# Weights for TensorE kept 128 bytes further into their buffers, and no 512 wide products

## The chip, the core and the metric

The kernel runs on one core of a Trainium2 chip. The metric is the device time of one execution in microseconds, the median over the runs shown. A core has TensorE (matrix products; PE in the profile, its weight loads PEld), VectorE (DVE), ScalarE (ACT), GpSimd (POOL) and SyncE (SP, which issues the DMAs here). Each works through its own queue in order and waits for the others by semaphores.

## The reference

A decoder trunk of two layers over 256 positions of width 2048, in float32. Layer 0 is a recurrent block (RG-LRU), layer 1 sliding-window attention with 32 query heads over 4 shared K/V heads; each is followed by a SwiGLU FFN of inner width 5632.

```python
def swiglu_ffn(x, g, w_in, w_out):
    h = rms_norm(x, g)
    gate, up = jnp.split(h @ w_in, 2, axis=-1)
    return x + (jax.nn.silu(gate) * up) @ w_out
...
    y_branch, x_branch = jnp.split(h @ w_in, 2, axis=-1)
    xb = causal_depthwise_conv(x_branch, conv_w, conv_b)
    hs = rg_lru(xb, w_rg, b_rg, w_ig, b_ig, lam)
    return x + (hs * jax.nn.gelu(y_branch)) @ w_out
...
    for layer in range(DEPTH):
        if layer < N_REC:
            x = recurrent_block(...)
        else:
            if layer == N_REC:
                k_band, v_band = shared_kv(x, kv_norm_g, w_kv, k_norm_g)
            x = attn_block(x, ..., k_band, v_band)
        x = swiglu_ffn(x, norm2_g[layer], ffn_w_in[layer], ffn_w_out[layer])
```

## The kernel before

Activations lie transposed: 128 features on the partitions, 256 positions along the free axis. A float32 number is used as a high part, rounded for TensorE's float32r format, and a low part, the rest. A product of weights W and activations X is then three products: high W with high X ("a" in the code), high W with low X ("b"), low W with high X ("l").

Weights come as tiles of 128x1024 (256 inputs by 512 outputs, 4096 bytes a partition), one DMA each on SyncE's queue into one of four raw buffers. `split` makes hi (ScalarE, line 363) and lo (VectorE, line 364) of it in one of four pairs of buffers; this runs three tiles ahead of TensorE. A job is one such tile: `stream` issues its load, the split of a later tile, then its products, and then as much background work (norms, gates, attention) as fits a budget of VectorE and ScalarE time. The order of all instructions is so fixed when the program is built.

Kinds of jobs:

- A plain group (`group`, products at line 411) has the 128x128 blocks of hi and lo as the stationary weights and the activations as the moving operand, 256 columns wide. A group is four banks (four blocks of 128 outputs) over all inputs; one weight tile gives 24 products, a group over 2048 inputs 192. The LRU's input projections, its output projection, FFN groups 0 to 3 and every second one from 5 on, and the FFN's output projection are such groups. Line 944 (the LRU's gates), line 578 (the attention's output projection in two of its groups, by turns with the heads) and line 1139 (K) use hi and lo as weights in the same way.
- A fast group (`fast_group`, line 606; FFN groups 4, 6, ... 20) saves products by Strassen-like sums (`mix`, lines 374 to 380). There hi and lo, and mixtures of them in slots, move, and the activations in slots are the stationary weights.
- In Q (line 1333) and V (lines 1148 to 1150) hi and lo move too, and the activations are the weights.

Runs of wide products: in the jobs that `sync` names (`SYNC`, mostly the first three of a group), three of the 16 pairs "a" and "b" are issued as one product "h" of 512 columns, high and low X side by side, one behind another. Its second half goes to columns 256 to 511 of the bank. So the first two banks of such a group hold two halves, and whoever reads them adds the halves: a copy by ScalarE into a tile t, an add by VectorE (`pull`, `residual`). 26 groups have such runs, 9 wide products each, and the first group has two more.

Where things lie in a partition matters to the change. SBUF tiles are laid out in the order in which `__init__` makes them. From hi0 to the last slot every tile's size is a multiple of 1024 bytes, but for a tile "step" of 64 bytes between slots 6 and 7. With r for the remainder of hi0's address by 512, all of hi and lo and the near slots (0 to 6) begin at r, the far slots (7 to 36) at r + 64. A 128x128 block of weights is 512 bytes, a 256 wide operand 1024 bytes, so every block and every half of a slot keeps its tile's remainder. Activations are taken from far slots; `mix` takes near slots for its results where job entry 2 is 1, and far slots where it is 2 (tiles 0 and 4 of a group). While a product runs, the weights of the next are loaded. "Spacing" below is the remainder by 512 of the address of those next weights less that of the running product's moving operand: -64 in the plain groups, +64 or (with a mixture in a far slot) 0 in the fast ones.

```python
self.jobs.append((src(c), mm, False))     # a job: source, products, 1 or 2 if mixed
...
run = [(0, 0), (1, 0), (0, 1)] if c in sync else []
todo = [(k, f, p) for k, f in both if (k, f) not in run for p in "ab"]
...
if i == self.NEAR:
    const.tile([P, 16], F32, name="step")
```

Of the kernel before, what the change touches and what calls it, by code (L numbers as in the profile page):

```python
# [49 lines left out]
class Trunk:  # L50
# [12 lines left out]
    SYNC = (0, 1, 2)  # L63
# [13 lines left out]
    def __init__(self, ctx, tc, dram):  # L77
# [276 lines left out]

    def split(self, i):
        raw, hi, lo = self.raw[i % 4], self.hi[i % 4], self.lo[i % 4]
# [28 lines left out]
    def stream(self):  # L385
        n = len(self.jobs)
        for i in range(-self.LD, n):
# [13 lines left out]
    PARTS = {"h": (1, 0, 2 * T), "a": (1, 0, T), "b": (1, T, 2 * T), "l": (0, 0, T)}  # L401

    def products(self, todo, ps, hi, lo, x2, begun, last):


        for n, (k, f, p) in enumerate(todo):
# [4 lines left out]
            self.nc.tensor.matmul(ps[f][:, 0:c1 - c0], w, x2[k][:, c0:c1], start=f not in begun,  # L411
# [3 lines left out]
    def group(self, src, nk, xs, done, last=False, sync=(), four=False, pre=None):  # L415
# [4 lines left out]
        for c in range(nk // 2):  # L420
            def mm(hi, lo, c=c):
# [23 lines left out]
                if c == nk // 2 - 1:  # L445
                    done([(p, bool(sync) and f < 2) for f, p in enumerate(st["ps"])])
            self.jobs.append((src(c), mm, False))

    def pull(self, bank, o=None, r=None):

        ps, two = bank
        o = self.half() if o is None else o
        if two:
            t = self.t()
            self.a(t, ps[:, T:2 * T])
            self.tt(o, ps[:, 0:T], t, ALU.add)
            if r is not None:
                self.tt(o, o, r, ALU.mult)
        elif r is not None:
# [74 lines left out]
    def residual(self, g, ps, gains, r, out=None, part=None):  # L534
        for f in range(4):
            xt = self.x[g][:, f, :]
            p, two = ps[f]
# [907 lines left out]
```

## Time and profile before

| what | value |
|---|---|
| median of 3 runs | 1959.46 us (1959.16 to 1964.55) |
| span of the profiled execution, first to last instruction | 1958.5 us |
| what lies around the span, against the median | 1.0 us |
| TensorE busy | 1953.4 us (100%) |
| VectorE, ScalarE busy | 1538.3 us (79%), 1142.0 us (58%) |
| read from HBM | 376.06 MB, 195 GB/s over the span |
| granted TensorE clock | 1.000 |

A row of a group reads: line, engine, operation, out<-in by the program's names, shape, xcount | busy us, mean ns of one | idle us before. For TensorE the first input named is the moving operand and the second the weights; "128*128" is the array, "128x256" the moving operand. A row of the timeline reads: start us, length us from the first start to the last end, engine, line, operation, names, shape of the first, xcount, and in brackets idle time before it. A row of the windows reads: stretch, its length, then busy us and in brackets the number of instructions that run in it for TensorE, its weight loads, VectorE, ScalarE and GpSimd, then granted clock, DMA share and GB/s.

### The profile page before, as it was taken

How to read it: one execution, taken by the hardware profiler on the slowest of the kernel's cores; microseconds unless marked ns; L12 is line 12 of the kernel's file. 1: busy time of each engine (PE TensorE's matmuls, PEld its weight loads, DVE VectorE, ACT ScalarE, POOL GpSimd, SP SyncE). 2: the span in 40 equal slices, each digit the busy share in tenths (PEclk: the TensorE clock that was granted, in tenths of full speed). 3: DMA queues.
4: the chain of work that ended last, by engine and by line, in shares of the span. 5: the costliest groups of instructions: out<-in, count | busy, mean ns of one | idle time of the engine just before them, and what ended most of it. 6: DMA issues, size and time to landing. Idle time of an engine off the chain costs nothing.

```text
span 1958.5 us, 40255 instructions
## 1 busy us (share of the span) xinstructions
PE 1953.4 (100%) x16516; PEld 1916.5 (98%) x16516; DVE 1538.3 (79%) x2477; ACT 1142.0 (58%) x1670; POOL 0.2 (0%) x4
## 2 busy tenths in 40 slices
PE   9999999999999999999999999999999999999999
PEld 9999999999999999999998899999999999999999
DVE  7989868989899998545667776798899988954443
ACT  7799756555555566444556775565555655744442
POOL 0000000000000000000000000000000000000000
DMA  7555665556666557555554335656566566666663
GB/s 283 188 184 197 212 218 186 188 200 208 205 203 204 204 196 247 194 194 194 194 185 149 130 119 185 208 188 205 194 205 205 202 208 204 230 205 204 205 205 127
DMA packets 107321, 384.97 MB, mean 197 GB/s; under 512 B 11904, under 2 KB 14080, under 8 KB 107136
## 3 DMA queue, kind: packets, MB, share of 16 engines
q1 hardware_dynamic: 106848, 381.99, 58.0%
q8 instruction: 129, 2.11, 0.4%
q14 instruction: 56, 0.46, 0.1%
q10 hardware_dynamic: 288, 0.40, 0.1%
HBM read 376.06 MB, written 6.29 MB: 195 GB/s over the span
## 4 chain that ended last, share of the span: by engine, by line
PE 95%; DVE 2%; DMA 1%; issue 1%; ACT 0%; DVEq 0%; ACTq 0%
PE b L411 67%; PE b L606 16%; PE b L1333 5%; PE b L578 2%; PE b L944 1%; DMA raw<-in_ffn_in 1%; PE b L1184 1%; DVE lo L364 1%; PE b L1248 1%; PE b L1229 1%; PE b L1139 1%; DVE s L144 0%; DVE lo L379 0%; PE b L802 0%; PE b L1307 0%
## 5 line engine op out<-in xcount | busy, mean ns | idle before, releaser
L411 PE MATMUL b<-s,hi 128*128 128x256 f32 (+1 forms) x7700 | 1021.5, 280 | 0.2
L411 PEld LDWEIGHTS b<-s,hi 128*128 128x128 f32 x7700 | 954.0, 188 | 10.9 <-DVE s L144 0.5
L364 DVE TENSOR_TENSOR lo<-raw,hi 128x1024 fp32r<-128x1024 f32 (+1 forms) x579 | 701.9, 1219 | 310.2 <-ACT hi L363 305.1
L363 ACT ACTIVATE hi<-raw 128x1024 fp32r<-128x1024 f32 (+1 forms) x579 | 607.5, 1055 | 457.9 <-PE b L411 396.5
L411 PE MATMUL b<-s,lo 128*128 128x256 f32 x3968 | 586.3, 276 | 0.0
L411 PEld LDWEIGHTS b<-s,lo 128*128 128x128 f32 x3968 | 512.4, 188 | 0.0
L378 ACT ACTIVATE s<-s 128x1024 fp32r<-128x1024 f32 x126 | 131.9, 1058 | 194.1 <-DVE s L377 194.0
L606 PE MATMUL b<-s,s 128*128 128x256 f32 x1512 | 196.2, 279 | 0.4 <-DVE s L380 0.4
L606 PEld LDWEIGHTS b<-s,s 128*128 128x128 f32 x1512 | 183.1, 189 | 0.6 <-DVE s L380 0.6
L606 PE MATMUL b<-hi,s 128*128 128x256 f32 x1044 | 178.0, 277 | 0.0
L380 DVE TENSOR_TENSOR s<-s,s 128x1024 fp32r<-128x1024 f32 x126 | 153.7, 1220 | 5.9 <-ACT s L378 5.9
L606 PEld LDWEIGHTS b<-hi,s 128*128 128x128 f32 x1044 | 152.4, 188 | 0.0
L606 PE MATMUL b<-lo,s 128*128 128x256 f32 x522 | 132.7, 277 | 0.2 <-DVE lo L364 0.2
L375 DVE TENSOR_TENSOR s<-raw 128x512 f32<-128x512 f32 x126 | 86.5, 686 | 47.0 <-DMA raw<-in_ffn_in 46.8
L135 ACT ACTIVATE s<-s 128x512 fp32r<-128x512 f32 (+3 forms) x177 | 87.4, 522 | 55.8 <-DVE s L144 40.3
L379 DVE TENSOR_TENSOR lo<-raw,hi 128x768 fp32r<-128x768 f32 x126 | 118.5, 951 | 0.0
L374 ACT ACTIVATE hi<-raw 128x768 fp32r<-128x768 f32 x126 | 102.4, 833 | 7.4 <-ACT s L378 3.6
L606 PEld LDWEIGHTS b<-lo,s 128*128 128x128 f32 x522 | 92.7, 188 | 0.4 <-DVE lo L364 0.4
L1333 PE MATMUL b<-hi,s 128*128 128x512 f32 x256 | 84.0, 408 | 0.0
L144 DVE TENSOR_TENSOR s<-s,s 128x512 fp32r<-128x512 f32 (+2 forms) x143 | 75.1, 551 | 1.7 <-ACT s L135 1.7
L135 ACT ACTIVATE s<-b 128x256 fp32r<-128x256 f32 (+4 forms) x132 | 57.5, 468 | 24.7 <-PE b L1248 7.2
L144 DVE TENSOR_TENSOR s<-b,s 128x512 f32<-128x512 f32 (+3 forms) x126 | 63.7, 531 | 4.2 <-ACT s L135 3.0
(117 smaller groups left out, 1208.1 us busy)
## 6 DMA issues: line engine op xcount, KB each, us to landing
raw<-in_ffn_in SPq DMA_DIRECT2D x352, 512.0 KB, 3.4
raw<-in_ffn_out SPq DMA_DIRECT2D x176, 512.0 KB, 4.2
raw<-in_lru_in SPq DMA_DIRECT2D x63, 512.0 KB, 3.6
raw<-in_lru_out SPq DMA_DIRECT2D x32, 512.0 KB, 4.1
raw<-in_w_q SPq DMA_DIRECT2D x32, 512.0 KB, 3.2
raw<-in_w_o SPq DMA_DIRECT2D x32, 512.0 KB, 3.3
raw<-in_gate SPq DMA_DIRECT2D x8, 512.0 KB, 4.2
away<-s SPq DMA_DIRECT2D x8, 512.0 KB, 3.4
```

What stands on the lines that cost most here:

```text
L135: self.nc.scalar.activation(out, in_, func, **kw)
L144: self.nc.vector.tensor_tensor(out, a, b, op)
L363: self.nc.scalar.activation(hi[:, q], raw[:, q], AF.Copy)
L364: self.nc.vector.tensor_tensor(lo[:, q], raw[:, q], hi[:, q].bitcast(F32), ALU.subtract)
L374: act(hi[:, q], raw[:, q], AF.Copy)
L375: tt(two(d[:, 0:2 * T]), two(raw[:, T:3 * T]), raw[:, 0:T].unsqueeze(1).to_broadcast([P, 2, T]), ALU.subtract)
L378: act(mh[:, :], d[:, :], AF.Copy)
L379: tt(lo[:, q], raw[:, q], hi[:, q].bitcast(F32), ALU.subtract)
L380: self.mark = tt(ml[:, :], d[:, :], mh[:, :].bitcast(F32), ALU.subtract)
L411: self.nc.tensor.matmul(ps[f][:, 0:c1 - c0], w, x2[k][:, c0:c1], start=f not in begun, stop=last and all(q[1] != f for q in todo[n + 1:]))
L606: nc.tensor.matmul(st["ps"][b][:, h % 2 * T:(h % 2 + n) * T], x, w, start=b not in st["begun"], stop=True, skip_group_check=True)
L1333: nc.tensor.matmul(st[g][b][:, :], x, q, start=c + kt == 0 and x is xh and q is wh, stop=c == 7 and kt == 1 and q is wl)
```

## The change

- hi and lo become 512 bytes longer (a partition holds 1024 + 128 numbers). `parts` gives the 1024 numbers to use: from number 32 on, 128 bytes in, where the job's third entry is None (hi and lo are stationary weights, and V, which shares its job with K), from 0 where it is a number (fast groups 0, 1 or 2; Q now 0). All hi and lo buffers keep one remainder, 4608 being 9 times 512. The plain groups, lines 578, 944 and 1139 so have the spacing +64, V has -64, fast groups and Q keep theirs. Behind a fast group's last product the next plain weights have the spacing 128, once.
- `SYNC`, `sync`, part "h" and the banks' second halves are gone: 236 products of 512 columns become 472 of 256, and 52 copies on ScalarE and 52 adds on VectorE leave.
- The zero tile of the warm-up products is hi[3]. The tiles in front of hi move by a little.

```diff
+    STEP = 32
-        self.zero = const.tile([P, P + T], F32R, name="zero")
-        self.hi = [const.tile([P, 1024], F32R, name=f"hi{i}") for i in range(4)]
-        self.lo = [const.tile([P, 1024], F32R, name=f"lo{i}") for i in range(4)]
+        self.hi = [const.tile([P, 1024 + P], F32R, name=f"hi{i}") for i in range(4)]
+        self.lo = [const.tile([P, 1024 + P], F32R, name=f"lo{i}") for i in range(4)]
...
+    def parts(self, i):
+        o = 0 if self.jobs[i][2] is not None else self.STEP
+        return (q[i % 4][:, o:o + 1024] for q in (self.hi, self.lo))
...
-                self.jobs[i][1](self.hi[i % 4], self.lo[i % 4])
+                self.jobs[i][1](*self.parts(i))
...
-                    todo[0:4] = [(0, f, "h") for f in range(2)]
...
-                    run = [(0, 0), (1, 0), (0, 1)] if c in sync else []
-                    todo = [(k, f, p) for k, f in both if (k, f) not in run for p in "ab"]
-                    at = sync.index(c) if run else 0
-                    todo[at:at] = [(k, f, "h") for k, f in run]
-                    todo += [(k, f, "l") for k, f in both]
+                    todo = [(k, f, p) for k, f in both for p in "ab"] + [(k, f, "l") for k, f in both]
...
-        if two:
-            t = self.t()
-            self.a(t, ps[:, T:2 * T])
-            self.tt(o, ps[:, 0:T], t, ALU.add)
...
-            if two:
-                t = self.t()
-                self.a(t, p[:, T:2 * T])
-                self.tt(xt, xt, t, ALU.add)
...
-            self.jobs.append((w[g, c], mm, False))       # of queries
+            self.jobs.append((w[g, c], mm, 0))
```

On TensorE, the first tile of layer 0's FFN stood so before (b is a bank, s the activations, hi_77 the weights, numbers are buffers):

```order
L411 MATMUL b_141<-s_2965,hi_77 128x512
L411 MATMUL b_142<-s_2965,hi_77 128x256 x2
L411 MATMUL b_143<-s_2965,hi_77 128x256 x2
L411 MATMUL b_141<-s_2965,hi_77 128x256 x2
L411 MATMUL b_140<-s_2965,hi_77 128x512 x2
L411 MATMUL b_142<-s_2965,hi_77 128x256 x2
L411 MATMUL b_143<-s_2965,hi_77 128x256 x2
L411 MATMUL b_140<-s_2965,lo_81 128x256
```

The bank that comes free last is b_140, and the products into the three others stand ahead of it. In the changed kernel the same place on TensorE (the last bank is b_139, the buffer hi_76):

```order
L416 MATMUL b_140<-s_3002,hi_76 128x256 x2
L416 MATMUL b_141<-s_3002,hi_76 128x256 x2
L416 MATMUL b_142<-s_3002,hi_76 128x256 x2
L416 MATMUL b_139<-s_3002,hi_76 128x256 x4
L416 MATMUL b_140<-s_3002,hi_76 128x256 x2
L416 MATMUL b_141<-s_3002,hi_76 128x256 x2
L416 MATMUL b_142<-s_3002,hi_76 128x256 x2
L416 MATMUL b_139<-s_3002,lo_80 128x256
```

Each 512 wide product has become two of 256 columns; six products go ahead of the last bank where the old order had one wide and six narrow ones.

On VectorE, just ahead of that tile, before: the residual adds of the LRU's last output group (s_137 is a quarter of the residual stream, b the banks, t the copied second halves) and the first activation made of it:

```order
L144 TENSOR_TENSOR s_137<-s_137,b_145 128x256
L144 TENSOR_TENSOR s_137<-s_137,b_146 128x256
L144 TENSOR_TENSOR s_137<-s_137,t_86 128x256
L144 TENSOR_TENSOR s_137<-s_137,b_147 128x256
L144 TENSOR_TENSOR s_137<-s_137,t_87 128x256
L144 TENSOR_TENSOR s_137<-s_137,b_140 128x256
L148 SCALAR_TENSOR_TENSOR s_3639<-s_137,par,s_3639 128x256
```

And in the changed kernel:

```order
L143 TENSOR_TENSOR s_136<-s_136,b_144 128x256
L143 TENSOR_TENSOR s_136<-s_136,b_145 128x256
L143 TENSOR_TENSOR s_136<-s_136,b_146 128x256
L147 SCALAR_TENSOR_TENSOR s_3673<-s_136,par,s_3673 128x256
L143 TENSOR_TENSOR s_136<-s_136,b_139 128x256
```

The two adds of second halves are gone, and the activation stands ahead of the last bank's add.

More of the change, by code (lines that the diff above doesn't have):

```diff
@@ L410, in products, with group @@
             w = (hi if high else lo)[:, k * 512 + f * P:k * 512 + f * P + P]
-            self.nc.tensor.matmul(ps[f][:, 0:c1 - c0], w, x2[k][:, c0:c1], start=f not in begun,
+            self.nc.tensor.matmul(ps[f][:, 0:T], w, x2[k][:, c0:c1], start=f not in begun,
                                   stop=last and all(q[1] != f for q in todo[n + 1:]))
             begun.add(f)
-    def group(self, src, nk, xs, done, last=False, sync=(), four=False, pre=None):
+    def group(self, src, nk, xs, done, last=False, four=False, pre=None):
         st = {}
@@ L445, in mm, with pull @@
                 if c == nk // 2 - 1:
[L446 to L451, printed above, removed]
+                    done(st["ps"])
+            self.jobs.append((src(c), mm, None))
+    def pull(self, ps, o=None, r=None):
         o = self.half() if o is None else o
-        if two:
-            t = self.t()
-            self.a(t, ps[:, T:2 * T])
-            self.tt(o, ps[:, 0:T], t, ALU.add)
-            if r is not None:
-                self.tt(o, o, r, ALU.mult)
-        elif r is not None:
+        if r is not None:
             self.tt(o, ps[:, 0:T], r, ALU.mult)
@@ L536, in residual @@
             xt = self.x[g][:, f, :]
-            p, two = ps[f]
+            p = ps[f]
             h = part or 0
             self.tt(xt, xt, p[:, h * T:h * T + T], ALU.add)
-            if two:
-                t = self.t()
-                self.a(t, p[:, T:2 * T])
-                self.tt(xt, xt, t, ALU.add)
             if part != 0:
@@ L581, in mm @@
                 if c == last:
-                    self.residual(g, [(p, False) for p in ps], gains, r, part=g)
-            self.jobs.append((w[g, c], mm, False))
+                    self.residual(g, ps, gains, r, part=g)
+            self.jobs.append((w[g, c], mm, None))
         for q in (range(last - 1), range(last - 1, last + 1)):
@@ L595, in done @@
                 self.residual(g, ps, gains, r, out)
-            self.group(lambda c, g=g: w[g, c], nk, xs, done, g == 3, () if out is not None and g == 3 else self.SYNC)
+            self.group(lambda c, g=g: w[g, c], nk, xs, done, g == 3)
     def fast_group(self, src, xn, mx, g, done, final):
@@ L813, in ffn @@
             if g < self.PLAIN:
-                self.group(src, ND, xs, start, g == self.PLAIN - 1, self.SYNC, four=True)
+                self.group(src, ND, xs, start, g == self.PLAIN - 1, True)
             elif g in self.FAST:
@@ L818, in ffn @@
                 end = g == self.FAST[-1] + 1
-                self.group(src, ND, xn, direct, g == NH // 2 - 1, (), True, 6 if end else None)
+                self.group(src, ND, xn, direct, g == NH // 2 - 1, True, 6 if end else None)
             if g == 0:
@@ L930, in done @@
                 self.spawn(task())
-            self.group(lambda c: w[4 + g, c], ND, xs, done, sync=self.SYNC if g == 2 else (3, 4, 5) if g == 0 else ())
+            self.group(lambda c: w[4 + g, c], ND, xs, done)
         def gates(n):
@@ L1034, in done @@
                 self.spawn(task())
-            self.group(lambda c: w[g, c], ND, xs, done, g == 3, self.SYNC if g else ())
+            self.group(lambda c: w[g, c], ND, xs, done, g == 3)
         for step in self.ORDER.split():
@@ L1052, in done @@
         def done(ps):
-            k0 = [self.pull((p, False)) for p in ps[:2]]
+            k0 = [self.pull(p) for p in ps[:2]]
             for b in range(2):
@@ L1368, in run @@
         self.spawn(first())
-        nc.vector.memset(self.zero[:, :].bitcast(F32), 0.0)
+        zero = self.hi[3]
+        nc.vector.memset(zero[:, 0:P + T].bitcast(F32), 0.0)
         p = self.bank()
         for _ in range(self.WARM):
-            nc.tensor.matmul(p[:, 0:T], self.zero[:, 0:P], self.zero[:, P:P + T], start=True, stop=True)
+            nc.tensor.matmul(p[:, 0:T], zero[:, 0:P], zero[:, P:P + T], start=True, stop=True)
         self.free_bank(p)
```

25 lines of the change are left out of this document (9 added, 16 removed).

## The prediction

> **What bounds the kernel now.** I read the page's head first, then the groups by form, then stretches of the timeline for the pace of TensorE.
>
> ```profile
> span 1958.5 us, 40255 instructions
> PE 1953.4 (100%) x16516; PEld 1916.5 (98%) x16516; DVE 1538.3 (79%) x2477; ACT 1142.0 (58%) x1670; POOL 0.2 (0%) x4
> PE 95%; DVE 2%; DMA 1%; issue 1%; ACT 0%; DVEq 0%; ACTq 0%
> L411 PE MATMUL b<-s,hi 128*128 128x256 f32 x7464 | 976.5, 276 | 0.1
> L411 PE MATMUL b<-s,lo 128*128 128x256 f32 x3968 | 586.3, 276 | 0.0
> L411 PE MATMUL b<-s,hi 128*128 128x512 f32 x236 | 67.4, 393 | 0.1
> ```
>
> TensorE runs without a break and is 95% of the chain that ended last, so the time is the sum of the distances from one product's start to the next. The 276 ns is one product's passage; products overlap, and what costs is the distance. It is read from stretches in which nothing but 256 wide products runs: width of the window over weight loads started in it.
>
> ```profile
> 7.75:24.01 16.26, 16.26 (x140) 16.25 (x138) 15.76 (x34) 14.61 (x30) 0.00 (x0) 1.00 0.95 380
> 307.64:316.01 8.37, 8.37 (x73) 8.37 (x72) 6.62 (x11) 3.97 (x6) 0.00 (x0) 1.00 0.46 157
> 753.19:758.73 5.54, 5.54 (x50) 5.54 (x48) 5.42 (x10) 3.56 (x6) 0.00 (x0) 1.00 0.57 195
> 1264.70:1274.47 9.77, 9.77 (x84) 9.77 (x84) 7.92 (x12) 5.66 (x8) 0.00 (x0) 1.00 0.50 164
> 765.29:818.78 53.49, 53.49 (x473) 53.49 (x472) 26.03 (x25) 20.89 (x21) 0.00 (x0) 1.00 0.61 198
> ```
>
> The second pair of figures is TensorE's products, the third its weight loads. The last row has 472 products in 53.49 us, 113.3 ns each; the first 138 in 16.26 us, 117.8 ns each. The same instruction with the same shapes has two paces, 4.45 ns apart, at the same granted clock (1.00 in all rows). Where the slow one begins and ends is read here:
>
> ```profile
> 305.74 1.07 PE L411 MATMUL b<-s,lo 128*128 128x256 f32 x8
> 307.08 0.50 PE L523 MATMUL b<-con,sq 128*128 128x1 f32 x4
> 309.41 1.10 PE L411 MATMUL b<-s,lo 128*128 128x256 f32 x8
> 316.01 2.04 PE L411 MATMUL b<-s,hi 128*128 128x512 f32 x13
> 317.89 1.10 PE L411 MATMUL b<-s,lo 128*128 128x256 f32 x8
> 320.66 1.07 PE L411 MATMUL b<-s,lo 128*128 128x256 f32 x8
> 752.63 0.60 PE L802 MATMUL b<-con,s 128*128 128x128 f32 x4
> ```
>
> Eight products take 1.07 us before the norm's small products at 307 us, (1.07 - 0.28) / 7 = 113 ns, and 1.10 us after them, 117 ns. The slow pace outlasts the group and the first run of 512 wide products (three of the 13 at 316 us) and is gone behind the second. The window at 753 us begins behind the transposes at 752.63 us in the same way. So a disturbance starts it and, in the lines that keep the weights in hi and lo, only the wide runs or a fast group end it.
>
> By the layout in the code, the product's moving tile and the weights loaded beside it stand -64 bytes apart (modulo 512; next weights minus moving tile) in all of these lines. Two other spacings occur. In fast groups hi and lo move and slots are the weights: +64, and 0 where the second mixture lies in a far slot.
>
> ```profile
> 381.46 1.60 PE L606 MATMUL b<-s,s 128*128 128x256 f32 x12
> L606 PE MATMUL b<-hi,s 128*128 128x256 f32 x1044 | 178.0, 277 | 0.0
> 389.15 0.39 PE L606 MATMUL b<-lo,s 128*128 128x256 f32 x2
> 391.19 0.39 PE L606 MATMUL b<-lo,s 128*128 128x256 f32 x2
> 430.84 0.50 PE L606 MATMUL b<-lo,s 128*128 128x256 f32 x2 [0.21 <-DVE lo L364]
> 431.18 0.62 PE L606 MATMUL b<-hi,s 128*128 128x256 f32 x4
> 431.86 0.62 PE L606 MATMUL b<-hi,s 128*128 128x256 f32 x4
> ```
>
> At 0 it is (1.60 - 0.28) / 11 = 120 ns. At +64, 18 products lie between 389.15 and 391.19 us: 113.3 ns, although 120 ns went before. After the stall at 430.84 us, six products take 431.86 - 431.18 = 0.68 us: 113 ns at once. So at +64 the fast pace comes back by itself where at -64 the slow one stays. The shared K/V stage has both in turn: its K products at -64, its V products at +64.
>
> ```profile
> 1001.50 0.40 PE L1139 MATMUL b<-s,hi 128*128 128x256 f32 x2
> 1002.44 0.28 PE L1139 MATMUL b<-s,lo 128*128 128x256 f32 x1
> 1002.79 0.28 PE L1150 MATMUL b<-hi,s 128*128 128x256 f32 x1
> 1003.82 0.28 PE L1150 MATMUL b<-hi,s 128*128 128x256 f32 x1
> 1003.93 0.39 PE L1139 MATMUL b<-s,hi 128*128 128x256 f32 x2
> 1005.18 0.28 PE L1139 MATMUL b<-s,lo 128*128 128x256 f32 x1
> 1005.41 0.28 PE L1149 MATMUL b<-lo,s 128*128 128x256 f32 x1
> 1006.59 0.28 PE L1150 MATMUL b<-hi,s 128*128 128x256 f32 x1
> ```
>
> K slow (8 products in 0.94 us), then V fast (9 in 1.03); K fast (11 in 1.25), then V slow (10 in 1.18): the phase that is slow at -64 is fast at +64, and the reverse. A disturbance leaves the first phase nearly always (the windows at 307 and 753 us, above), so at +64 it should leave the fast pace. But a slow pace at +64 exists, and holds for ten products.
>
> **The change, part by part.** Sums go against the profiled span of 1958.5 us; the runs' median of 1959.46 us is 1.0 us more, for what lies around the span.
>
> *Spacing.* Weights go from remainder r to r + 128, far slots stay at r + 64: -64 becomes +64 for lines 411, 578, 944 and 1139 (K). Products now slow: in line 411 the four windows hold 339 (138, 71, 47 and 83 started inside), and 14 shorter stretches, mostly of 19 products between wide runs, hold 265: 604 in all (the first and, but for a single product, the last of the 14 are shown). In line 578 (the output projection by turns, which has no wide runs), the median passage is 279 ns where the fast one is 276, and 343 of its 384 are slow; line 944 has 23, line 1139 42.
>
> ```profile
> L578 PE MATMUL b<-s,hi x256: 276/279/388, 1147.1 to 1207.1; 128*128 128x256 f32 x128
> 24.71:26.95 2.24, 2.24 (x21) 2.24 (x20) 2.24 (x7) 1.98 (x5) 0.00 (x0) 1.00 0.68 230
> 1275.17:1277.41 2.24, 2.24 (x20) 2.23 (x19) 2.24 (x7) 1.69 (x3) 0.00 (x0) 1.00 0.50 188
> ```
>
> (604 + 343 + 23 + 42) x 4.45 ns = 4.5 us, all on the path. V goes from +64 to -64: now half slow, then half slow again, nothing. The bounds for a product at the new spacing are 113.3 (fast groups) and 117.8 ns (V's slow half); I take 113.3, since the 1,044 products that move hi in the fast groups have a mean passage of 277 ns with stalls and 120 ns neighbours among them, far nearer to 276 than to 279.
>
> *Wide products.* 236 of them become 472. A wide one is 393 - 276 = 117 ns longer than a narrow one, the second narrow one costs 113.3: 236 x 3.7 ns = 0.9 us gained. Their service, ending a slow stretch, goes too; that is the rivals' matter.
>
> *Second halves.* Each of 26 groups drops two copies on ScalarE and two adds on VectorE.
>
> ```profile
> L144 DVE TENSOR_TENSOR s<-s,t 128x256 f32<-128x256 f32 x26 | 11.0, 421 | 1.6
> L148 DVE SCALAR_TENSOR_TENSOR s<-s,par,s 128x256 fp32r<-128x256 f32 x80 | 36.7, 479 | 0.9 <-ACT s L135 0.9
> 293.74 1.01 PEld L411 LDWEIGHTS b<-s,hi 128*128 128x128 f32 x6 [0.27 <-DVE s L144]
> 1252.06 1.01 PEld L411 LDWEIGHTS b<-s,hi 128*128 128x128 f32 x8 [0.28 <-DVE s L144]
> ```
>
> Some 20 us of VectorE go (52 adds of about 0.4 us) and as many copies on ScalarE, beside TensorE, so nothing, but for two places: the first FFN products of each layer wait 0.27 and 0.28 us for a bank that VectorE's residual adds free. By the orders shown with the change, two adds of 0.42 us leave ahead of that free and an activation of 0.48 us moves ahead of it, 0.36 us earlier; but six products stand ahead of that bank in place of one wide and six, so it is wanted some 0.23 us earlier too. About 0.13 us of each wait goes (bounds: nothing, and all 0.27): 0.3 us gained. The stall in the first fast group (0.21 us at 430.84) has VectorE behind its own split of a weight tile, not behind what is removed; I leave it, with nothing and its own length as bounds.
>
> *Warm-up.* The zero tile becomes hi[3]: the memset is the same size, and the fourth tile's split waits for the warm-up products, done at 6.7 us, while ScalarE is still busy with the first tile then. Nothing.
>
> Sum: 4.5 + 0.9 + 0.3 = 5.7 us, 1958.5 to 1952.8 us, as a median 1953.8 us, 0.29% less. What this measurement can tell from no change is about 0.3%, or 5.9 us (1953.6 us): the forecast lies on that line.
>
> The page "SBUF — State Buffer" of the Trainium skill says, under "Who interferes with whom", that TensorE's two read ports are independent and that TensorE never waits for anyone. By that no spacing would matter; 120 ns at spacing 0 against 113.3 at +64 in one fast group speaks against it, and the first rival is worked out without it.
>
> **The rivals.**
> 1. *Spacing is not the cause*: each disturbance starts the slow pace at +64 as at -64, and no wide run ends it. Then it stands from the start to the first fast group (3,258 products by the groups' sizes, 24 for each weight tile), from 753 us through the first FFN's output (2,160), and from 1147 us to the second layer's fast groups (1,536): 6,954 x 4.45 = 30.9 us, less the 4.5 that are slow now and the 1.2 of the other terms: +25 us, 1985 us. For it: the wide runs do end slow stretches today. Against: the fast groups return by themselves.
> 2. *A slow stretch without an end* (slower): the phases are two at either spacing, V shows both, and one entry in some ten goes the other way. Places: behind the transposes at 752.6 us and their like in layer 1, each ahead of 2,160 products with nothing between: 9.6 us apiece. One gives 1963 us, both 1973 us. Or behind the 18 passages from a fast to a plain group, where one product has the spacing 128 that no row shows: 192 x 4.45 = 0.85 us each, 15 us for all, 1969 us. From 5.7 us / 4.45 ns = 1,280 slow products on, the change loses; from 2,600 on, by over 0.3%.
> 3. *Less is gained*: some lesser stretch stays slow (one of the LRU's stages of 400 to 1,200 products, 2 to 5 us), 1955 to 1959 us.
>
> **How the numbers follow.** All fast: 0.62, with its own range from 1951.5 (that stall gone as well, and others like it) to 1955.5 us; it falls on both sides of the 0.3% line, two thirds below, since the whole of the waits and of the stall at 430 us may go. Rival 3: 0.14. Rival 2 with one long stretch: 0.10; with more: 0.06. Rival 1: 0.08. Faster by over 0.3%: 0.40. Within: 0.22 + 0.14 + 0.10 = 0.46. Slower: 0.14. The range 1951.5 to 1963.5 us leaves out the last two, 0.14, and a little below.
>
> **What would show it.** Right: windows in the LRU, FFN output and output projection stages with 113.3 ns a product, behind the norms too; line 578's successor at a median passage of 276 ns; a first FFN product's wait of 0.15 us or less; products up by 236. Wrong: long stretches at 117.8 ns; where they begin (behind transposes, norms, or each fast group) tells rival 1 from rival 2.

## The result, and the profile after

The changed kernel is slower: 1975.72 us median (1973.47 to 1980.71, six runs) against 1960.15 us (1959.16 to 1964.55, six runs) for the kernel before, a ratio of 1.0077 with the 95% interval 1.0065 to 1.0088. 1953.8 us was forecast. The profiled execution took 1974.12 us, its span is 13.4 us longer than the one before, and its granted clock 1.000. One execution of the twelfth experiment below, at a granted clock of 0.942, took 2028.70 us and is in none of the figures.

The page's head, the engines' share of the chain and the plain groups' products:

```profile
span 1971.9 us, 40633 instructions
...
PE 1965.9 (100%) x16752; PEld 1938.4 (98%) x16752; DVE 1525.7 (77%) x2425; ACT 1131.7 (57%) x1620; POOL 0.2 (0%) x4
...
PE 96%; ACT 2%; DVE 1%; issue 0%; DVEq 0%; ACTq 0%
...
L416 PE MATMUL b<-s,hi 128*128 128x256 f32 x7936 | 1030.5, 278 | 1.4 <-ACT s L134 1.4
...
L416 PE MATMUL b<-s,lo 128*128 128x256 f32 x3968 | 590.4, 277 | 0.0
```

TensorE still never rests, with 236 products more, as the change says. VectorE and ScalarE lost 12.6 and 10.3 us (some 20 each were worked out ahead; neither is on the path). But the mean passage of a plain product rose from 276 to 278 and 277 ns, and 1.4 us of idle time stand ahead of line 416 (which was line 411), put down to ScalarE. The pace by stretches (width, then TensorE's products and its weight loads; one load in each count was already running when the window began and is left out below):

```profile
7.57:43.84 36.27, 36.27 (x322) 36.27 (x321) 32.46 (x68) 28.87 (x52) 0.00 (x0) 1.00 0.86 309
308.85:381.38 72.53, 72.53 (x642) 72.53 (x641) 66.80 (x121) 43.18 (x54) 0.00 (x0) 1.00 0.58 189
402.99:425.36 22.37, 22.37 (x193) 22.37 (x191) 18.75 (x27) 10.86 (x13) 0.00 (x0) 1.00 0.66 218
445.61:467.99 22.38, 22.38 (x193) 22.38 (x191) 19.02 (x27) 10.78 (x13) 0.00 (x0) 1.00 0.63 208
761.50:1005.16 243.66, 243.66 (x2152) 243.66 (x2151) 133.08 (x151) 111.11 (x133) 0.00 (x0) 1.00 0.59 195
```

The start (36.27 us / 320), the stretch behind the norm (72.53 / 640) and the first FFN's output behind its transposes (243.66 / 2150) run at 113.3 ns, where the kernel before was slow after each such disturbance. The two rows between are plain groups that follow fast groups: 22.37 / 190 = 117.7 ns. All 18 are so from the second product to their end (in the last group of each layer to its transposes); here is the first passage:

```profile
402.19 0.96 PE L595 MATMUL b<-s,s 128*128 128x256 f32 x7
402.99 0.98 PE L416 MATMUL b<-s,hi 128*128 128x256 f32 x7
```

Seven products of the fast group take (0.96 - 0.28) / 6 = 113 ns each, seven of the plain group (0.98 - 0.28) / 6 = 117 ns. Product by product, 3,340 are slow in these 18 groups (16 x 191 and 2 x 142), 14.9 us. Outside them 145 slow products of lines 416, 567 and 927 are left, where the kernel before had 961 in its lines 411, 578 and 944. In the turns' line 567 the median passage (the second of three figures) is the fast one; and in the timeline the first FFN products' weight loads no longer wait:

```profile
L567 PE MATMUL b<-s,hi x256: 276/276/388, 1154.8 to 1214.1; 128*128 128x256 f32 x128
```

```profile
295.45 1.25 PEld L416 LDWEIGHTS b<-s,hi 128*128 128x128 f32 x9
```

A second loss is new: TensorE waits behind the LRU's gates (line 927) for banks that ScalarE's sigmoids free (waits: us in all, times, longest; then the timeline).

```profile
PEld b L416 <- ACT s L134: 2.0, 3, 0.9
```

```profile
127.92 0.28 PE L927 MATMUL b<-s,lo 128*128 128x256 f32 x1
128.44 0.75 PE L416 MATMUL b<-s,hi 128*128 128x256 f32 x3 [0.24 <-ACT s L134]
...
185.01 0.28 PE L927 MATMUL b<-s,lo 128*128 128x256 f32 x1
185.98 0.38 PE L416 MATMUL b<-s,hi 128*128 128x256 f32 x1 [0.69 <-ACT s L134]
```

The distances are 0.52 and 0.97 us where 0.11 is due, and the products behind come at the pace of the sigmoids. On ScalarE, at the like place at 156 us, first the changed kernel and then the one before:

```profile
150.94 1.01 ACT L134 ACTIVATE s<-s 128x256 f32<-128x256 f32 x3
153.25 0.75 ACT L134 ACTIVATE s<-h 128x256 f32<-128x256 f32 x2 [1.30 <-DVE h L143]
153.91 1.05 ACT L368 ACTIVATE hi<-raw 128x1024 fp32r<-128x1024 f32 x1
...
156.27 1.57 ACT L134 ACTIVATE s<-b,par 128x256 f32<-128x256 f32 x4
```

```profile
150.30 1.01 ACT L135 ACTIVATE s<-s 128x256 f32<-128x256 f32 x3
151.22 0.63 ACT L135 ACTIVATE t<-b 128x256 f32<-128x256 f32 x2
151.75 1.05 ACT L363 ACTIVATE hi<-raw 128x1024 fp32r<-128x1024 f32 x1
...
154.11 1.57 ACT L135 ACTIVATE s<-b,par 128x256 f32<-128x256 f32 x4
```

Where the two copies of second halves (t<-b) stood, two squares of the y group's output (s<-h) now stand; they wait 1.30 us for VectorE's h, and the split and the four sigmoids behind them start 2.2 us later.

Summed over the trace, against the kernel before: slow products of lines 416, 567 and 927 +11.2 us (15.5 now, 4.3 then), wide products -0.9, irregular distances in the plain groups and gates +3.2 (4.8 now), stalls in a fast group (at 430 and 440 us) that are no longer there -1.1, the warm-up at the start +0.8, all else +0.2: together the 13.4 us.

### The profile page after: what moved, and what is told of

It is laid out like the page before. It is cut to its first block, busy times and chain, and to the rows that moved or that the text cites. A ratio compares the mean times of both kernels' runs of the same rounds, so it can differ in the third digit from the quotient of the medians.

```text
span 1971.9 us, 40633 instructions
## 1 busy us (share of the span) xinstructions
PE 1965.9 (100%) x16752; PEld 1938.4 (98%) x16752; DVE 1525.7 (77%) x2425; ACT 1131.7 (57%) x1620; POOL 0.2 (0%) x4
## 4 chain that ended last, share of the span: by engine, by line
PE 96%; ACT 2%; DVE 1%; issue 0%; DVEq 0%; ACTq 0%
PE b L416 67%; PE b L595 18%; PE b L1316 5%; PE b L567 2%; PE b L1167 1%; ACT s L134 1%; PE b L1231 1%; DVE lo L369 1%; PE b L1212 1%; PE b L1122 1%; ACT hi L368 1%; PE b L785 0%; DVE s L147 0%; ACT L134 0%; PE b L1290 0%
## 5 line engine op out<-in xcount | busy, mean ns | idle before, releaser
L416 PE MATMUL b<-s,hi 128*128 128x256 f32 x7936 | 1030.5, 278 | 1.4 <-ACT s L134 1.4
L416 PEld LDWEIGHTS b<-s,hi 128*128 128x128 f32 x7936 | 971.7, 188 | 2.7 <-ACT s L134 2.0
```

The costliest lines, as they stand in the source:

```text
L416: self.nc.tensor.matmul(ps[f][:, 0:T], w, x2[k][:, c0:c1], start=f not in begun, stop=last and all(q[1] != f for q in todo[n + 1:]))
```

## The experiments

"Passage" is the spacing of the one product on which a fast group ends and a plain group's first weights are loaded. Each ratio is to the kernel before, with its 95% interval.

**1. The 18 groups back at offset 0.**

```diff
-            self.jobs.append((src(c), mm, None))
+            self.jobs.append((src(c), mm, None if c == pre or c - 1 == pre else near))   # near = 0 behind fast groups
```

> The changed kernel, but the 18 plain groups that stand behind a fast group keep their weights at offset 0 (spacing -64, entered through spacing 0 for one product, as in the kernel before); the last two tiles of the last such group in each layer, behind the transposes, are at +64. Theory A (the entry through spacing 128 sets the slow pace, and nothing in the group ends it): those groups hold 3,340 slow products in the changed kernel, at 4.45 ns each 14.9 us; all of it goes, so some 15 us less than the changed kernel, within 2 us of the kernel before, and each passage from line 595 to line 416 is followed by 113.3 ns a product. Rival B (the slow pace comes from the wide runs that no longer stand in the stages ahead, or from something else of the changed kernel, and not from the entry): the groups stay at 117.8 ns and the time at 15 us over the kernel before.

1970.45 us, 1.0052 (1.0037 to 1.0067). The groups are fast, the first FFN's output is not:

```profile
403.00:424.54 21.54, 21.54 (x193) 21.54 (x191) 17.65 (x25) 10.00 (x12) 0.00 (x0) 1.00 0.61 206
754.04:1007.26 253.22, 253.22 (x2152) 253.22 (x2151) 135.81 (x155) 113.42 (x136) 0.00 (x0) 1.00 0.58 191
```

21.54 / 190 = 113.4 ns, 253.22 / 2150 = 117.8 ns. So 14.9 us went and 9.6 us came: the transposes in layer 0's last group turned the pace, which had been slow ahead of them, into the fast one before, and here a fast one into the slow one. Theory A holds for the groups; its time did not, since it left this out.

**2. The planner's budgets charged as if the second halves were read** (336 ns for VectorE and 313 for ScalarE at each of the 52 former reads).

> The changed kernel, with the planner's budgets charged as if the banks' second halves were still copied and added, so that the background work stands (but for small moves) where it stood in the kernel before; no instruction comes back. Theory C1 (the new waits of 0.4 to 0.9 us behind the LRU's gates at 128, 156, 182 and 185 us come from background work on ScalarE and VectorE that moved ahead of the gates' sigmoids): these waits go, 4 us less than the changed kernel. Theory C2 (they come from the order of the products: with wide runs at a group's head the third and fourth bank were wanted some 0.4 and 0.2 us later): the waits stay, and the time is that of the changed kernel within 1 us. The 18 slow groups stay slow by either.

1977.36 us, 1.0088 (1.0067 to 1.0109), runs at 1973.5, 1974.1, 1980.6 and 1981.6 us. The profiled one, 1981.57 us, was slow from the start to 302 us (37.69 / 320 = 117.8 ns), some 2,490 products or 11 us, and at that pace had no such waits. So the two theories are not told apart. But the spread of the runs has a likely reason: the start leaves one pace or the other, and 11 us less the waits of 3 to 4 are about the 7 us by which runs of this and of the changed kernel differ. The runs without a profile can't show it.

```profile
7.63:45.32 37.69, 37.69 (x323) 37.69 (x321) 32.48 (x68) 28.89 (x52) 0.00 (x0) 1.00 0.82 301
```

**3. No offset, no wide runs** (`STEP = 0`).

> The changed kernel with no offset (STEP = 0): all plain groups at the spacing -64, and no wide runs. Theory A: the 18 groups behind fast ones are fast again (14.9 us less), but each disturbance ahead of a stretch without fast groups leaves the slow pace at -64 and nothing ends it: from the start to the first fast group (3,258 products), the first FFN's output (2,160), and the second layer's head (1,536), 6,954 x 4.45 = 30.9 us; so the kernel before and about 25 to 31 us. Rival B (spacing plays no part, wide runs alone made the difference): as the changed kernel, 15 us over the kernel before. A third possibility, that at -64 the slow pace ends by itself too once nothing wide is there: about the time of the kernel before.

1984.68 us, four runs within 0.2 us, 1.0125 (1.0108 to 1.0142): 25 us, the first theory's figure. 6,884 products of lines 416, 567 and 927 are slow (6,954 were counted ahead), the 18 groups fast.

**4. The offset with the wide runs kept.**

> The kernel before with the offset alone: weights 128 bytes in as in the changed kernel (and the zero tile in hi[3]), wide runs and second halves kept. Theory A: the 18 groups behind fast ones are slow (14.9 us more; they hold no wide runs), the slow stretches at -64 are gone (4.5 us less), and the waits behind the gates are not there: the kernel before and about 10 us. Rival B (losing the wide runs is what made the groups slow): no slow group, 4 to 5 us less than the kernel before.

2006.32 us, 1.0236 (1.0221 to 1.0251): neither theory. 11,081 products of its plain groups are slow, 49 us. Behind the transposes the pace is fast until the first wide run of the next group, and slow behind it:

```profile
770.34:775.44 5.10, 5.10 (x48) 5.10 (x46) 4.98 (x9) 3.23 (x6) 0.00 (x0) 1.00 0.57 191
782.01:837.47 55.46, 55.46 (x471) 55.42 (x470) 25.07 (x23) 20.69 (x21) 0.00 (x0) 1.00 0.57 190
```

5.10 / 45 = 113.3 ns, 55.46 / 469 = 118 ns. So the wide runs do not end a slow pace as such. At +64 a run of three turned a fast pace slow nine times of nine; at -64, in the kernel before, it ended a slow one in nine cases of 18. It is as if they set one phase, which is fast at -64 and slow at +64, though not every time.

**5. The passage at +64**, by a far slot for the last fast tile's mixture.

```diff
-            self.jobs.append((src(c), mm, (c in self.PAIRS) + (c in self.EVEN)))
+            self.jobs.append((src(c), mm, (c in self.PAIRS) + (c in self.EVEN or c == 7)))
```

> The changed kernel, but in the fast groups the last tile's second mixture lies in a far slot too, so the next plain weights stand +64 from it: the passage to a plain group goes from spacing +64 to +64 without the one product at 128. Twelve products more in each of 18 fast groups stand at spacing 0 (18 x 12 x 6.7 ns = 1.4 us). Theory A1 (the product at spacing 128 sets the slow pace): the 18 groups run at 113.3 ns, 14.9 - 1.4 = 13.5 us less than the changed kernel. Theory A2 (the passage from moving weights to moving activations sets one phase whatever the entry's spacing, and that phase is the slow one at +64): the groups stay at 117.8 ns, 1.4 us more than the changed kernel.

1978.26 us, 1.0086 (1.0071 to 1.0101). Slow (22.38 / 190 = 117.8 ns): a group can be slow without a product at the spacing 128, against A1's forecast. It does not clear that spacing, though: here the twelve products just ahead of the passage stand at spacing 0, and eight such products leave the slow pace at +64 in experiments 13 and 14 below.

```profile
448.93:471.31 22.38, 22.38 (x193) 22.38 (x192) 18.48 (x26) 10.58 (x13) 0.00 (x0) 1.00 0.59 193
```

**6. Only the first tile of the 18 groups at offset 0** (`None if c else near`).

> The changed kernel, but the first of the eight tiles of each of the 18 plain groups behind fast ones is at offset 0 (spacing -64, entered through 0, as before), the other seven at +64. Theory A3 (there are two phases, each fast at one of the two spacings and slow at the other, as K and V showed; the phase is carried along and only a disturbance changes it): first tiles at 113.3 ns, all tiles behind them at 117.8 ns; 18 x 24 products become fast, 1.9 us less than the changed kernel. Rival (only a product at spacing 128 does the harm, and what is fast stays fast): all 192 products fast, 14.9 us less.

1968.35 us, 1.0038 (1.0023 to 1.0053). All 192 products fast, the first 24 at -64 and the rest at +64; the first FFN's output slow again. So a fast pace is carried from -64 to +64, against A3.

```profile
444.00:465.53 21.53, 21.53 (x192) 21.53 (x191) 18.15 (x26) 10.34 (x12) 0.00 (x0) 1.00 0.61 205
```

**7 and 8. Offsets of 256 and 384 bytes** (`STEP = 64` and `96`).

> The changed kernel with the weights 256 bytes in (STEP = 64): spacing 192 in plain groups, 256 at the 18 entries. Theory A4 (two paces exist only where weights and moving tile are nearer than some bound, as at 64 on both sides): no 117.8 ns stretch, all plain groups at one pace; if it is 113.3 ns, 15 us less than the changed kernel. Rival (two phases at every spacing but 0): the 18 groups, or the stretches behind norms and transposes, slow, anything from 0 to 35 us over an all-fast 1960 us.

> The changed kernel with the weights 384 bytes in (STEP = 96): spacing -192 in plain groups, -128 at the 18 entries. Theory A4 and its rival as for 256 bytes; in addition, if the sign of the spacing decides which phase is the fast one (A3), this kernel is slow where the one with +192 is fast and the reverse: the sum of the two kernels' slow products would then be about all of the plain groups' products.

1984.72 us, 1.0122 (1.0105 to 1.0139), and 1975.50 us, 1.0079 (1.0061 to 1.0097). The first is the kernel without offset over again (1984.68 us), the second the changed kernel (1975.72 us). A plain group of each, behind a fast one:

```profile
413.09:434.62 21.53, 21.53 (x192) 21.53 (x191) 17.58 (x25) 10.02 (x12) 0.00 (x0) 1.00 0.63 203
```

```profile
406.13:428.50 22.37, 22.37 (x192) 22.37 (x191) 18.91 (x27) 10.88 (x13) 0.00 (x0) 1.00 0.65 220
```

113.3 and 117.7 ns. The behaviour repeats every 256 bytes; no offset tried is free of the two paces, so A4 falls.

**9. The first tile of the LRU's groups ordered bank by bank** (`for f in range(4) for k in range(2)` in its high products).

> The changed kernel, but the first tile of each of the LRU's input groups has its high products ordered bank by bank (four products a bank, 0.45 us) in place of two a bank (0.23 us); a sigmoid that frees a bank takes 0.39 us. Theory C2 (the waits behind the gates come from the order of the products, which wants banks faster than ScalarE frees them): the 30 products of 222 ns behind each wait go, and the first waits shorten, 2.5 to 4 us less than the changed kernel with the same pace at the start (1974 us in such runs). Theory C1 (background work stands ahead of the sigmoids and holds the first bank): the first waits of 0.4, 0.6, 0.4 and 0.9 us stay, and at most the 2.3 us behind them go.

1977.05 us, 1.0085 (1.0066 to 1.0103). Its waits at 127.4 and 184.5 us stay (0.50 and 0.93 us); in its slow stretch from 128 to 179 us there were none. C2 is not borne out.

**10 and 11. Passage 0 into +64, and passage 128 into -64**, by shifting the last fast tile's hi and lo.

```diff
-        o = 0 if self.jobs[i][2] is not None else self.STEP
+        o = {None: self.STEP, 3: 32}.get(self.jobs[i][2], 0)     # 96, with the groups at offset 0, in the other
...
-        near = self.jobs[i][2] == 1
+        near = self.jobs[i][2] != 2
...
-            if c in self.EVEN:
+            if c in self.EVEN or c == 7:                         # products with hi and lo last
...
-            self.jobs.append((src(c), mm, (c in self.PAIRS) + (c in self.EVEN)))
+            self.jobs.append((src(c), mm, 3 if c == 7 else (c in self.PAIRS) + (c in self.EVEN)))
```

> The changed kernel, but the last tile of each fast group has its hi and lo 128 bytes in as well and its products in the order that ends with them: the passage to the plain group then has the spacing 0, and the plain group behind it +64. Theory H1 (what counts is the passage: at 0, and as the kernel with 256 bytes showed at 256, the pace behind it is the fast one, at any other it is the slow one): the 18 groups run at 113.3 ns, 14.9 us less; the transposes in the last group of layer 0, which turned a slow pace into a fast one and a fast into a slow one so far, then leave the first FFN's output slow, 9.6 us more; 5 us less than the changed kernel in all. Theory H2 (what counts is the plain group's own spacing: behind a fast group -64 and 192 are fast, +64 and -192 slow, whatever the passage): the groups stay at 117.8 ns and the time at that of the changed kernel.

> The kernel with the 18 groups at offset 0 (first experiment), but with the last fast tile's hi and lo 384 bytes in and its products in the order that ends with them: the passage has the spacing 128, the plain group behind it -64. Theory H1: the 18 groups are slow (14.9 us more than the first experiment's 1970 us), the first FFN's output is then fast (9.6 us less). Theory H2: the groups stay at 113.3 ns and the time at the first experiment's.

1970.25 us, 1.0051 (1.0036 to 1.0066), and 1977.93 us, 1.0083 (1.0066 to 1.0100). First two windows of the one, then a window of the other:

```profile
444.81:466.12 21.31, 21.31 (x191) 21.31 (x189) 16.74 (x24) 9.39 (x10) 0.00 (x0) 1.00 0.59 192
756.40:1009.62 253.22, 253.22 (x2152) 253.22 (x2151) 136.19 (x156) 112.80 (x136) 0.00 (x0) 1.00 0.57 191
```

```profile
406.79:429.16 22.37, 22.37 (x192) 22.37 (x191) 18.46 (x27) 10.75 (x12) 0.00 (x0) 1.00 0.62 214
```

At +64 the group is fast behind passage 0 (21.31 / 188 = 113.4 ns), at -64 slow behind passage 128 (22.37 / 190 = 117.7 ns): H1 as forecast, in all 18 groups of both, with the turn at layer 0's transposes too. But the nine products just ahead of the passage, in which the shifted hi and lo move at the spacings -64 and 192, are slow already in both kernels (in the second 1.06 us from 448.51 to 449.57, 117.8 ns each). So its plain groups may only carry on a pace that stood ahead of the passage, and that 128 did anything there is not shown; in the first the pace does turn at the passage, from slow to fast. Over the kernels so far: passage 0 or 256, fast (six, with the kernel before); 64, 128 or -128, slow (seven, with the changed kernel). Where the fast group ended in the fast pace, as in all of them but the fifth's and these two, that is shown for 0, 256, 128 and -128. The second kernel's time exceeds its forecast, as its LRU was slow (1,351 products, 6 us, less the waits that a slow pace covers).

**12. First tiles at offset 0, last groups left at +64, bank by bank order.**

> The changed kernel with three mendings: the first tile of 16 of the 18 groups at offset 0 (all 192 products were fast that way), the last group of each layer left at +64 and so slow ahead of its transposes (in all kernels so far the transposes turned a slow pace into a fast one, ten times out of ten), and the bank by bank order in the LRU. From the 1968.3 us of the sixth experiment: 9.6 us less for the first FFN's output, 1.3 more for the two last groups, up to 4 less in the LRU: 1957 to 1960 us, at or below the kernel before. If the turn at the transposes is chance, the first FFN's output stays slow and the time is 1966 to 1969 us.

1964.29 us, 1.0020 (1.0011 to 1.0030), between its two forecasts. The last group is slow up to the transposes and the first FFN's output fast behind them, as forecast (243.67 / 2150 = 113.3 ns); but 960 products of the LRU are slow at 117.8 ns, and the waits behind the gates stay.

```profile
757.90:1001.57 243.67, 243.67 (x2152) 243.67 (x2151) 134.75 (x153) 111.25 (x133) 0.00 (x0) 1.00 0.59 197
185.52:298.58 113.06, 113.06 (x960) 113.06 (x961) 83.61 (x138) 70.30 (x115) 0.00 (x0) 1.00 0.60 206
```

**13 and 14. Low products at spacing 0 as a reset, at +64**, without and with the charged budgets.

```diff
+        at = {None: (self.STEP, self.STEP), "z": (self.STEP, 16)}.get(self.jobs[i][2], (0, 0))
+        return (q[i % 4][:, o:o + 1024] for q, o in zip((self.hi, self.lo), at))
...
+            self.jobs.append((src(c), mm, "z" if c in zero else None if c else near))     # zero: (0,), mostly
```

> The changed kernel with the first tile of 16 of the 18 groups at offset 0, the last group of each layer at +64, and, in the first tile of every plain group outside the FFNs' second parts (and two further tiles, behind the start and behind the FFN's norm), lo 64 bytes in: its eight low products then stand at the spacing 0 (8 x 6.7 ns = 54 ns a group, some 1.5 us in all). Theory H1 (a product at spacing 0 leaves the fast pace behind it, whatever was ahead): the start, the LRU and the first FFN groups are slow for one tile at most behind each disturbance, in every execution; of line 416's slow products only the 284 of the two last groups and some 200 others are left; the waits behind the gates (about 4.5 us) stay: 1961 us, and the runs lie within 1 us of one another. If a product at spacing 0 does this only on the passage from a fast group: long slow stretches in the LRU as in the fourteenth of these comparisons' like, 1964 to 1968 us, spread over 5 us and more.

> The kernel with the low products at spacing 0, and the planner's budgets charged as in the second experiment, so that the background work stands where it stood in the kernel before. Theory C1 (background work that moved ahead of the gates' sigmoids is what TensorE waits for there): the waits at 128, 156, 182 and 185 us go, 4 us less than the kernel without the charge, 1957 us, which is below the kernel before by 0.1 to 0.2%. If the waits come only from TensorE being earlier at that place than in the kernel before, they stay, and so does the time, 1961 us.

1994.61 and 1994.54 us, 1.0170 (1.0156 to 1.0184) and 1.0169 (1.0155 to 1.0183), each kernel's runs within 0.8 us. H1 does not hold beyond the passage: behind each run of eight such products the pace is the slow one, where ahead of some it was fast.

```profile
214.15:235.82 21.67, 21.67 (x186) 21.67 (x185) 19.97 (x38) 15.01 (x25) 0.00 (x0) 1.00 0.64 215
```

21.67 / 184 = 117.8 ns. It is what the wide runs did in the fourth experiment, and with it the spread of the runs is gone. The waits were covered by the slow pace in both, so C1 stayed open.

**15. The kernel before, with the offset in line 578's jobs alone.**

> The kernel before with the offset of 128 bytes in the output projection by turns alone (line 578; 48 jobs' worth of products, no wide runs there before either). Its 343 slow products of 384 become 34 to 110 as in the changed kernel: 1.0 to 1.4 us less than the kernel before, the 18 groups and the LRU as they were. If the group behind it, entered from +64 to -64, then runs slow up to its first wide run, 0.1 us of that is given back.

1961.48 us, 1.0000 (0.9991 to 1.0008): no difference. The turns' median passage is 276 ns, as forecast, a gain of 1.1 us that this measurement cannot tell. The kernel before spreads by 4 us itself; the profile here shows one reason. Behind a stall of 0.6 us at 440 us a fast group runs slow to its end (30 products at 117.7 ns, at +64), and the plain group behind it is slow too (22.38 / 190 = 117.8 ns), in spite of passage 0; a stall of 0.5 us at 483 us does the same to the next fast group and the plain group behind it. So the passage at 0 did not make the pace here: a group entered fast stayed fast (the other 16), one entered slow stayed slow. And the fast pace does not always come back by itself at +64: in the kernel before, behind a stall of 0.6 us at the same place, it was back after three products.

**16 and 17. The reset at -64**, without and with the charged budgets: plain groups at offset 0, lo 64 bytes in for 17 tiles, the turns at +64.

> No wide runs, no offset (spacing -64) but for line 567's jobs by turns (+64), and a reset by spacing: in 13 first tiles of groups that stand behind a disturbance (LRU groups, the first output group of each projection, the first FFN group, and three further tiles behind the start and the norms) lo lies 64 bytes in, so that eight low products stand at spacing 0 (54 ns a tile, 0.9 us in all). At +64 such products left the slow pace behind them each time, in every execution. Theory H3 (they set one phase, as the wide runs do, which is slow at +64 and fast at -64): at -64 the fast pace stands behind each of them; of the 6,884 slow products that the kernel without offset and wide runs showed, some 500 are left, 1984.7 - 28.4 + 0.9 = 1957 us if the LRU's waits do not come back, 1961 us if they do, with runs within 1 us or so of one another. If they leave the slow pace whatever the spacing: 1985 us and more.

> As the kernel with the reset by spacing at -64, and the planner's budgets charged as if the second halves were still read. Theory C1 (moved background work is what TensorE waits for behind the gates): no waits of 0.4 us and more at 128, 156, 182 and 185 us here and such waits there, 4 us between the two, and 1957 us here. If TensorE's earlier arrival alone makes the waits: the same waits and the same time in both.

1969.83 us, 1.0051 (1.0038 to 1.0063), and 1969.93 us, 1.0052 (1.0038 to 1.0065). Windows of the first, ahead of a reset, behind it, and in the first FFN's output:

```profile
45.52:54.47 8.95, 8.95 (x77) 8.95 (x77) 6.90 (x11) 5.34 (x6) 0.00 (x0) 1.00 0.53 172
55.31:74.13 18.82, 18.82 (x169) 18.82 (x167) 18.82 (x36) 11.35 (x17) 0.00 (x0) 1.00 0.58 182
763.92:1008.90 244.98, 244.98 (x2082) 244.98 (x2081) 127.08 (x143) 104.97 (x124) 0.00 (x0) 1.00 0.56 189
```

Slow (8.95 / 76 = 117.8 ns), then fast (18.82 / 166 = 113.4): H3, that such products set one phase as the wide runs do, fast at -64, holds through the LRU, most of the first FFN groups and the second layer. Not every reset works: in the first FFN's output the only one failed in both kernels, 9.3 us, and in the first kernel that at 298 us too. With the pace held, the charge takes 0.3 us of the waits, of some 4:

```profile
PEld b L416 <- ACT s L134: 1.5, 2, 0.9
```

```profile
PEld b L416 <- ACT s L134: 1.2, 2, 0.7
```

```profile
152.90 0.75 ACT L134 ACTIVATE s<-h 128x256 f32<-128x256 f32 x2 [1.30 <-DVE h L143]
```

The last row, of the second kernel, says where they come from: the squares still stand ahead of the sigmoids and wait for VectorE. So charging the budgets alone does not move them back.

**18. The LRU's input groups as before, resets elsewhere.** Wide runs and copies in these groups alone; behind them none, with three to five resets in each projection.

> The LRU's input groups as in the kernel before (wide runs, second halves read by ScalarE's copies), everything behind them without wide runs, with the reset by spacing at -64 (the first tile of each group of the projections, the second tile too in a projection's first group, two tiles of the first FFN group) and line 567's jobs at +64. Theory C1 (in the changed kernel two squares of an LRU group's output moved into the place on ScalarE's queue that the two copies held, ahead of the gates' sigmoids, and wait 1.3 us there for VectorE): with the copies back the squares stand behind the sigmoids, and the waits at 156, 182 and 185 us go, 4 us less than the kernel with the reset at -64 (1969.8 us). Theory H3: with four to five resets in the first FFN's output, its 2,146 slow products become 600 or fewer, 7 us less or more. Both: 1957 to 1959 us, below the kernel before by up to 0.15%; the waits alone: 1966 us; neither: 1970 us.

1958.15 us, runs from 1957.46 to 1958.90, 0.9985 (0.9976 to 0.9994): below both kernels, as forecast.

```profile
151.96 0.64 ACT L135 ACTIVATE t<-b 128x256 f32<-128x256 f32 x2
...
154.85 1.57 ACT L135 ACTIVATE s<-b,par 128x256 f32<-128x256 f32 x4
...
156.61 0.28 PE L950 MATMUL b<-s,lo 128*128 128x256 f32 x1
156.73 0.96 PE L417 MATMUL b<-s,hi 128*128 128x512 f32 x4
```

```profile
763.93:819.92 55.99, 55.99 (x496) 55.99 (x495) 26.97 (x28) 22.81 (x25) 0.00 (x0) 1.00 0.61 197
```

With the copies back in their place the sigmoids start 1.9 us ahead of the group that wants their banks, and the group follows at 0.12 us: no wait. The first FFN's output is fast (55.99 / 494 = 113.3 ns) from its second reset on; the first, behind the transposes, failed here too. The copies and the order of the wide products came back together here; that the copies alone would do was not run.

## Why the prediction was wrong

- *Spacing* (4.5 us gained): its first half held. At +64 the start, the norms and the transposes left the fast pace in the profiled execution, and line 567 went to a median of 276 ns: 961 slow products became 145 outside the 18 groups, 3.6 us. The step that failed is the price of a product at the new spacing: 113.3 ns was taken for all, since the fast groups' products were near it. Those are products in which hi moves; a plain group behind them is another case. Its passage at 128 was named in the second rival ("behind the 18 passages", 15 us, 1969 us) and given a part of 0.06. It came whole: 3,340 products at 117.8 ns, 14.9 us, and the first and sixth experiments show that the way into the group makes them, as with the group's first tile back at offset 0 all its products are fast. K and V had shown that a pace can turn where the moving operand changes; the passage should have been priced as one case, 18 times alike, not as a chance in ten.
- The rival's chance spoke of one entry in some ten; in fact each passage at 64, 128 or -128 had a slow group behind it, in every kernel. And that at +64 the fast pace "comes back by itself" was read from one stall; two stalls in the fifteenth experiment's profile show the contrary.
- *First rival*: its working came out for a kernel at -64 (1984.68 us in the third experiment, 1985 worked out). Its premise was not true of +64 in most runs, though the start went slow in some.
- *Second halves* ("beside TensorE, so nothing"): mis-sized by some 3 us. Their going gained nothing, but their places on ScalarE's queue were filled by squares that wait for VectorE, ahead of sigmoids for which TensorE waits. The last experiment has the copies back there and no wait, but the wide products too, so the cause of this part is argued in part.
- *Wide products*, 0.9 us: 236 more products, as said. Their service was put into the rivals alone; the fourth experiment shows that at +64 they do harm.
- *First FFN products* (0.3 us): held, no idle time is left there. *Warm-up* ("nothing"): the 30 warm-up products took 0.8 us longer, 6.1 against 5.4 us. That is most likely chance: in the 18 experiments, which all have hi[3] as the zero tile, they took from 5.2 to 6.4 us, by how many of them came 213 ns apart.
- The rule cited from the Trainium skill's page "SBUF — State Buffer", "Who interferes with whom", that TensorE's two read ports are independent and TensorE never waits on anyone, would make spacing indifferent. These runs disagree: by the addresses of the weights alone the same products come 113.3 or 117.8 ns apart at one clock, 14.9 us here and 46 us in the fourth experiment.

## What to carry to other kernels

Where one engine is the bound and a pace of it depends on how streams fall together, an entry into each stage is a case of its own: price the first product of a stage as a switch for all that follow, and look for a row with that same entry before taking a neighbour's price. Instructions that cost nothing may still hold a place in an in-order queue; when they leave, ask what moves up there and whom that waits for. A reset at a known price (here eight products at 120 ns, or a wide run), put where the pace behind it is the fast one and repeated in case one fails, gave a narrower and lower time than a layout that is fast only if the last disturbance left it so.

## What the runs showed of the hardware

- A 256 wide product with its weight load takes 113.3 or 117.8 ns from start to start at the same clock, and some 120 ns at spacing 0. Which of the first two it is can be carried along over two thousand products and more.
- Spacings that differ by 256 bytes behave alike: -64 and 192, 64 and -192 (1984.68 and 1984.72 us, 1975.72 and 1975.50 us). Of the spacings held over several products, 0 alone has 120 ns.
- Runs of 512 wide products, or of eight products at spacing 0, mostly set the pace: fast behind them at -64, slow at +64. Eight products at spacing 0, at -64 (experiments 16 to 18): 31 of 31 runs that met a fast pace kept it, 18 of 23 that met a slow one ended it. At +64 (13 and 14) the pace behind each was slow.
- Behind a fast group that ended fast, one product at 0 or 256 left the plain group fast and one at 128 or -128 left it slow, each time. The two groups that were entered slow through 0, at -64 (experiment 15), stayed slow.
- The transposes in layer 0's last group turned the pace in each kernel followed, either way; those of layer 1 left the fast one each time. Why, and what in the reads makes the 4.45 ns, stays open.
